# Two layers' causal convolution: one more of four channel tiles per layer as TensorE products (five tiles of eight)

## The chip, the cores and the metric

One core of one Trainium2 chip. The metric is the device time of one execution in microseconds (us), as the median of several runs; less is better. The engines are named TensorE (PE in the profile; its weight loads are PEld), VectorE (DVE), ScalarE (ACT), GpSimd (POOL) and SyncE (SP, which only issues transfers here). Each engine works through its own list of instructions in order; semaphores join them.

## What is computed

512 tokens of width 1024 go through two layers of a conformer-like block (16 learned tokens stand in front, so a layer works on L = 528 positions; the second layer needs only the last 512, T = 512), and then through one block with windowed attention, gated linear attention and 16 experts. All of it is float32. A layer of the first block, cut to what matters:

```python
a, g, zc, q, k, v, za, qi, ki, wi = split(h @ w_in[l])
u = a * sigmoid(g)                                   # [528, 512]
u = causal_conv(u, conv_w[l], width=31, per channel) + conv_b[l]
y_conv = silu(layer_norm(u)) * silu(zc)
y_attn = sparse_attention(q, k, v, qi, ki, wi, topk=132) * silu(za)
h = layer_norm(alpha * h + concat(y_conv, y_attn) @ w_out[l])
```

The convolution is depthwise: each of the 512 channels has 31 taps of its own, and reaches 30 positions back. The attention chooses 132 keys per query by a score of its own (`qi`, `ki`, `wi`).

## The kernel before, in words

The activations lie transposed, 128 channels on the partitions and the positions along the row, as a high and a low float32r part. A projection of 128 output channels (`proj`, line 164) is 8 blocks of the contraction times 3 products (high by high, low by high, high by low) times 2 column pieces: 48 matmuls at line 182 into one of two rotating accumulators named `pp`. Its weights are loaded by SP into one of three `raw` buffers, and split into `wh` on ScalarE (line 160) and `wl` on VectorE (line 161).

`layer` (line 281) writes a layer down phase by phase in the order `seq` of the plan (lines 75 to 86). `idx`, `sc` and `topk` are the key selection, with `topk` wholly on VectorE; `q`, `k`, `v`, `za`, `zc` are projections; `att` is the attention, one query block of 128 after another in four steps and more; `agN` computes the gated input of convolution tile N. A framework decides what comes first on each engine: every instruction has a priority by its level (`go`), the levels are ordered by the first tuple of the plan, and the framework lays out each engine's list by priority among what is ready in a simulation that it makes while it builds. In layer 0 `w`, `topk` and `tail` come ahead of `idx`, `proj`, `conv`, `att`, `ag`, `rest`; in layer 1 `w` and `tail` come ahead of `idx`, `conv`, `proj`, `att`, `ag`, `topk`, `rest`. Buffers of one name ("tag") rotate in the order in which the program is written, whatever the priorities are.

A convolution tile is 128 channels. `p_ag` (line 378) makes two projections (`a` and `g`), a tanh `th` on ScalarE (line 385) and one multiply on VectorE (line 386), which writes the tile's input `u`. The last entry of the plan, `pconv`, says which tiles then go tap by tap; their projections stand at level `ag`, those of the others at `proj`:

- Tap by tap (`conv_tap`, line 328): for each of 31 taps ScalarE scales a shifted view of `u` by the tap into one of two `prod` buffers (line 333), and GpSimd adds it to `cv` (line 335). The first tap writes `cv` itself, with the bias. So a tile is 31 activations and 30 adds.
- As products (`conv_operands`, line 341, and `conv_products`, line 363): the 128 channels are four groups of 32. TensorE spreads the taps over partitions with 16 small matmuls (line 346), VectorE turns them into diagonal weights `cwt` (line 348, buffer `k2l`). SP writes `u` to DRAM (`ud`, line 354) and reads it back four times per group, each time shifted by one position more, onto the four quarters of the partitions (`us` in the buffer of `szc`, line 359, and `side`, line 360). Then eight products per group, each of four taps for 32 channels, add up in `pp`; the four groups' products write four quarters of 32 output channels. These are two bursts (one per half of the columns) of 32 matmuls each (`burst`, lines 253 to 267, so they appear at lines 261 and 267), and ScalarE takes the result to `cv` with the bias (line 376). An fp32 product leaves two records in the trace.

Before, layer 0 makes tile 3 as products and tiles 0, 2 and 1 tap by tap (tile 0 at the very start of the layer, 2 and 1 during attention); layer 1 makes tiles 2 and 3 as products and 1 and 0 tap by tap, during attention.

The tail follows (line 712). First comes a warm-up: ScalarE reads the last tile of the sequence (`clast`, line 713, used at line 722) and then computes a square root (line 723), so that the table for it is loaded. Then `cv` is transposed (line 727), copied (`xct`, line 729) and measured (line 730), normalised, transposed back (line 754), passed through silu (line 755) and multiplied by `szc` (line 756) into `ych` and `ycl`. `xct` takes over buffers named `pT` that attention uses before. The attention output is multiplied into the gate `sza` (line 551) and split into `yah` and `yal`. The output projection (`w_out`, from line 766) reads `yah`, `yal` first and `ych`, `ycl` after them. Attention itself: scores on TensorE (`pidx`), mask and maximum on VectorE (`smb`, `mx`, lines 646 and 648), exponentials on ScalarE (line 651), transposes (line 616), copies (line 618) and products with the values (`po`).

Of the kernel before, what the change touches and what calls it, by code (L numbers as in the profile page):

```python
# [69 lines left out]
class Net:  # L70
    def __init__(self, tc, I, out, dbg=None, upto=99):
        self.tc, self.nc, self.I, self.out, self.dbg = tc, tc.nc, I, out, dbg
        self.upto = upto
        self.bgq = []
        self.plan = [
            (('w', 'topk', 'tail', 'idx', 'proj', 'conv', 'att', 'ag', 'rest', 'fill'),
             ('ag0', 'idx', 'q', 'k', 'sc', 'ag3', 'v', 'cp3', 'ag2', 'ag1', 'topk', 'zc', 'att', 'za'),
             (2, 0, 1, 3),
             (2, 3, 1, 0),
             (0, 1, 2)),  # L80
            (('w', 'tail', 'idx', 'conv', 'proj', 'att', 'ag', 'topk', 'rest', 'fill'),
             ('idx', 'q', 'k', 'sc', 'ag2', 'v', 'cp2', 'ag3', 'ag1', 'cp3', 'ag0', 'topk', 'att', 'za', 'zc'),
             (2, 0, 1, 3),
             (2, 3, 1, 0),
             (0, 1)),
        ]
        self.order2 = ('w', 'crit', 'att', 'gla', 'main', 'late', 'fill')
        self.gn0, self.apull, self.gpull, self.ng = 2, 3, (1, 0, 2, 1), 0
        self.early = ("qk", "qk", "u", "szc", "cv", "qi", "xl", "xl", "parts", "v", "c1", "sm", "sm", "one", "raw", "raw", "raw", "hw", "hl")
        self.last = ("raw", "u", "szc", "qi")  # L90
        self.cycle = ("qk", "qk", "u", "szc", "cv", "qi", "xl", "xl", "v", "sm", "sm", "one", "raw", "raw", "raw", "hw", "hl")
        self.piece = 264
        self.swap = True
        self.stack = True
        self.sqsum, self.sqe, self.xlp = 'v', 'AAAAAAAA', ()
        self.pairs2 = False
        self.pairs, self.spare = False, None
        self.cur = None
        self.pos = 0
# [181 lines left out]
    def layer(self, l):  # L281
# [46 lines left out]
        def conv_tap(c, j):  # L328
            src = u[:, c, j + 1 + q0:j + 1 + q0 + T]
            if not prod:  # L330
                prod.append(self.sb([128, 2, L], "prod", "zM"))
            pr = prod[0][:, j % 2, :T] if j else cv[:, c, :]
            nc.scalar.activation(pr, src, AF.Identity, scale=taps[:, c, j + 1:j + 2], bias=0.0 if j else cvec[:, c, 31:32])  # L333
            if j:
                nc.gpsimd.tensor_tensor(cv[:, c, :], cv[:, c, :], pr, op=ALU.add)  # L335
# [5 lines left out]
        def conv_operands(c):  # L341
            nx = T + W31 + 1 - CQ
            pt = self.ps([128, 4, 8], "pcv")
            for g in range(4):
                for k in range(CQ):
                    nc.tensor.matmul(pt[32 * k:32 * k + 32, g, :], self.ident[:, 32 * g:32 * g + 32], taps[:, c, k::CQ], start=True, stop=True)
            w = self.sb([128, 4, 8, 32], "cwt", "k2l")
            nc.vector.tensor_tensor(w.rearrange("p g e c -> p (g e) c"), self.mask32[:, None, :].to_broadcast([128, 32, 32]),
                                    pt.rearrange("p g e -> p (g e)")[:, :, None].to_broadcast([128, 32, 32]), op=ALU.mult)

            ust = self.sb([128, 3, nx], "us", "szc")
            us = [ust[:, g, :] for g in range(3)] + [self.side[:, 32:32 + nx]]
            ud = self.dram.tile([128, PAD + L], F32, name=f"ud{l}{c}")
            nc.sync.dma_start(ud, u[:, c, :])
            ug = ud.rearrange("(g p) x -> p g x", g=4)
            for k in range(CQ):
                p = slice(32 * k, 32 * k + 32)
                x0 = k + q0
                nc.sync.dma_start(ust[p], ug[:, 0:3, x0:x0 + nx])
                nc.sync.dma_start(us[3][p], ug[:, 3, x0:x0 + nx])  # L360
            ready[c] = w, us

        def conv_products(c):
            self.go("proj")
            n = T // 2
            w, us = ready.pop(c)
            ps = self.ps([128, 2, 512], "pp", "pp", 2)
            for k in range(2):
                products = []
                for e in range(8):  # L370
                    for g in (3, 2, 1, 0):
                        x0 = CQ * e + n * k
                        products.append(((ps[32 * g:32 * g + 32, k, :n], w[:, g, e, :], us[g][:, x0:x0 + n]),
                                         dict(start=e == 0, stop=e == 7, skip_group_check=True)))
                self.burst(products)
            nc.scalar.activation(cv[:, c, :].rearrange("p (k n) -> p k n", k=2), ps[:, :, :n], AF.Identity, scale=1.0, bias=cvec[:, c, 31:32])

        def p_ag(c):
            self.go("ag" if c in pconv else "proj")
            ps = []  # L380
            for n in ("a", "g"):
                raw = self.load_w(w_in, WCOL[n] + 128 * c, 128)
                ps.append(self.proj(self.split_w(raw), 128, hT, KT, fsegs))
            th = self.sb([128, L], "th", "rl", 3)
            nc.scalar.activation(fseg(th), ps[1], AF.Tanh, scale=0.5)  # L385
            nc.vector.scalar_tensor_tensor(fseg(u[:, c, PAD:]), fseg(th), 1.0, ps[0], op0=ALU.add, op1=ALU.mult)
            if c not in pconv:
                conv_operands(c)
                return
            self.go("conv")  # L390
            for j in range(W31):
                conv_tap(c, j)
# [112 lines left out]
        v = self.sb([128, 4, 512], "v")  # L505
# [199 lines left out]
                tmp = self.sb([128, T], "th", "rl", 3)  # L705
                self.silu2(seg(szc[0][:, e, :]), ps, seg(tmp))

        phases = dict(cp2=lambda: conv_products(2), cp3=lambda: conv_products(3), ag0=lambda: p_ag(0), ag1=lambda: p_ag(1), ag2=lambda: p_ag(2), ag3=lambda: p_ag(3), idx=p_idx, sc=p_scores, topk=p_topk, k=p_k, q=p_q, v=p_v, att=p_att, za=p_za, zc=p_zc)
        for n in seq:
            phases[n]()  # L710

# [73 lines left out]
        sc = self.sb([128, 5, 2], "sc")  # L785
# [1008 lines left out]
```

## Time and profile before

| | |
|---|---|
| Time, median of 3 runs | 1838.72 us (1835.46 to 1839.21) |
| The profiled execution, own time | 1837.06 us |
| Its span from the first to the last instruction | 1835.2 us |
| TensorE busy, share of the span | 1688.8 us, 92% |
| VectorE / ScalarE / GpSimd busy | 931.9 / 766.7 / 219.8 us |
| Mean granted TensorE clock | 0.970 of full speed |
| Layer 0 / layer 1 / the rest, about | 0 to 400 / 400 to 740 / 740 to 1835 us |

Numbers in the profile are microseconds from the start of the span unless marked ns. A matmul's record is longer than the distance to the next one, since they overlap; the distance is what a stream of them takes. "Idle before" is time in which an engine did nothing, with what ended it: `3.31 <-DVE mx L646` says that it waited 3.31 us until VectorE's instruction of line 646 that writes `mx`. Idle time of an engine that is not the bottleneck costs nothing.

### The profile page before, as it was taken

What the parts mean: (1) busy time and instruction counts of PE and PEld (TensorE: products, weight loads), DVE (VectorE), ACT (ScalarE), POOL (GpSimd) and SP (SyncE); (2) the same over time, 40 slices, a digit from 0 to 9 for tenths busy, and PEclk for the clock granted to TensorE, in tenths of its full rate; (3) what the DMA queues carried; (4) which work ended last, traced back from release to release, by engine and by line L of the source; (5) the groups of instructions that cost most, each with busy time, mean ns of one, the idle gap of its engine ahead of it and who ended that gap; (6) DMA issues with size and microseconds to landing.
All of it is one profiled execution on the core that took longest, in us unless ns stands there. A gap on an engine that the chain in (4) does not pass through costs nothing.

```text
span 1835.2 us, 28863 instructions
## 1 busy us (share of the span) xinstructions
PE 1688.8 (92%) x11867; PEld 1320.9 (72%) x11867; DVE 931.9 (51%) x1860; ACT 766.7 (42%) x1314; POOL 219.8 (12%) x161
## 2 busy tenths in 40 slices
PE   6999998989999999799999999998899988788888
PEld 6988896989987879798978899997533333233246
DVE  3899756566995556875534455544311221012044
ACT  3883587356526783643456453323200000000026
POOL 1620486000005740000000000000000000000000
PEclk9999998989999999899999999999999999999999
DMA  6124120121233112222113248466699999999961
GB/s 195 58 70 113 47 70 24 53 71 47 76 97 110 47 47 70 81 92 68 58 47 98 78 158 296 131 247 252 240 420 421 421 420 421 419 420 421 418 272 46
DMA packets 149461, 327.63 MB, mean 179 GB/s; under 512 B 13467, under 2 KB 103259, under 8 KB 131025
## 3 DMA queue, kind: packets, MB, share of 16 engines
q1 hardware_dynamic: 144464, 314.75, 46.7%
q10 hardware_dynamic: 3856, 7.37, 1.1%
q0 software_dynamic: 1008, 3.67, 0.5%
q8 instruction: 93, 1.52, 0.3%
q14 instruction: 40, 0.32, 0.1%
HBM read 308.58 MB, written 17.11 MB: 177 GB/s over the span
## 4 chain that ended last, share of the span: by engine, by line
PE 64%; DMA 17%; ACT 7%; DVE 6%; POOL 3%; issue 2%; ACTq 0%; DVEq 0%; POOLq 0%; SPq 0%
PE pp L182 41%; PE pp L1643 8%; DMA rawe<-in_w_exp_up 6%; DMA rawe<-in_w_exp_down 5%; DMA rawe<-in_w_exp_gate 4%; POOL cv L335 3%; PE pp L1703 2%; ACT wh L160 1%; ACT prod L333 1%; ACT smb L651 1%; PE pidx L242 1%; PE psc L1541 1%; PE po L261 1%; PE pidx L243 1%; DVE wl L161 1%
## 5 line engine op out<-in xcount | busy, mean ns | idle before, releaser
L335 POOL TENSOR_TENSOR cv<-cv,prod 128x528 f32<-128x528 f32 (+1 forms) x150 | 212.9, 1420 | 452.9 <-ACT prod L333 444.8
L1643 PE MATMUL pp<-rawe,xf 128*64 128x512 f32 x1024 | 251.0, 606 | 11.1 <-DMA rawe<-in_w_exp_gate 6.9
L160 ACT CAST wh<-raw 128x1024 fp32r<-128x1024 f32 (+2 forms) x149 | 151.0, 1016 | 253.1 <-PE pp L182 221.2
L182 PE MATMUL pp<-hTh,wh 128*128 128x264 f32 (+2 forms) x1056 | 223.3, 291 | 12.0 <-ACT th L385 9.8
L161 DVE TENSOR_TENSOR wl<-raw,wh 128x1024 fp32r<-128x1024 f32 (+2 forms) x149 | 186.6, 1253 | 92.1 <-ACT wh L160 81.9
L182 PE MATMUL pp<-hTl,wh 128*128 128x264 f32 (+2 forms) x1056 | 221.7, 289 | 0.0
L182 PE MATMUL pp<-hTh,wl 128*128 128x264 f32 (+2 forms) x1056 | 219.9, 287 | 0.0
L1643 PEld LDWEIGHTS pp<-rawe,xf 128*64 128x64 f32 x1024 | 78.4, 139 | 158.7 <-issue 133.0
L182 PEld LDWEIGHTS pp<-hTh,wh 128*128 128x128 f32 (+1 forms) x1056 | 165.4, 190 | 22.1 <-ACT th L385 12.2
L182 PEld LDWEIGHTS pp<-hTl,wh 128*128 128x128 f32 (+1 forms) x1056 | 165.7, 189 | 6.0 <-issue 5.5
L182 PEld LDWEIGHTS pp<-hTh,wl 128*128 128x128 f32 (+1 forms) x1056 | 165.5, 190 | 4.5 <-issue 4.0
L182 PE MATMUL pp<-xTh,wh 128*128 128x264 f32 (+1 forms) x752 | 153.7, 285 | 2.9 <-ACT op L1072 2.3
L182 PE MATMUL pp<-xTl,wh 128*128 128x264 f32 (+1 forms) x752 | 154.9, 285 | 0.7 <-DVE xTl L1167 0.7
L182 PE MATMUL pp<-xTh,wl 128*128 128x264 f32 (+1 forms) x752 | 154.5, 283 | 0.0
L1643 PE MATMUL pp<-rawe,hid 128*64 128x512 f32 x512 | 127.8, 617 | 19.1 <-DMA rawe<-in_w_exp_down 18.7
L1532 DVE SCALAR_TENSOR_TENSOR Y<-pp,per,Y 128x512 fp32r<-128x512 f32 x16 | 12.0, 748 | 233.5 <-ACT Y L1531 233.5
L333 ACT ACTIVATE prod<-u,taps 128x528 f32<-128x528 f32 (+1 forms) x150 | 107.3, 729 | 36.5 <-POOL cv L335 35.9
L1500 POOL DMA_INDIRECT xr<-xrows,slots x7 | 6.7, 958 | 938.8 <-DMA pled<-pe 639.4
L182 PEld LDWEIGHTS pp<-xTh,wh 128*128 128x128 f32 (+1 forms) x752 | 115.2, 189 | 4.6 <-ACT op L1072 2.5
L182 PEld LDWEIGHTS pp<-xTl,wh 128*128 128x128 f32 (+1 forms) x752 | 115.0, 188 | 3.6 <-issue 2.5
L182 PEld LDWEIGHTS pp<-xTh,wl 128*128 128x128 f32 (+1 forms) x752 | 115.1, 188 | 0.8 <-issue 0.8
L1643 PEld LDWEIGHTS pp<-rawe,hid 128*64 128x64 f32 x512 | 40.2, 141 | 100.6 <-issue 62.7
(526 smaller groups left out, 2941.7 us busy)
## 6 DMA issues: line engine op xcount, KB each, us to landing
rawe<-in_w_exp_gate SPq DMA_DIRECT2D x53, 1024.0 KB
rawe<-in_w_exp_up SPq DMA_DIRECT2D x52, 1024.0 KB
rawe<-in_w_exp_down SPq DMA_DIRECT2D x51, 1024.0 KB
raw<-in_w_in SPq DMA_DIRECT2D x45, 1024.0 KB
rawe<-in_w_exp_down SPq DMA_DIRECT2D x26, 512.0 KB
rawe<-in_w_exp_up SPq DMA_DIRECT2D x22, 512.0 KB
rawe<-in_w_exp_gate SPq DMA_DIRECT2D x22, 512.0 KB
raw<-in_w_in SPq DMA_DIRECT2D x20, 512.0 KB
```

What stands on the lines that cost most here:

```text
L160: nc.scalar.copy(wh, raw_view)
L161: nc.vector.tensor_sub(wl, raw_view, wh.bitcast(F32))
L182: nc.tensor.matmul(ps[:m, s, x:min(x + k, n)], a[:, t, :m], b[:, c0 + x:min(c0 + x + k, c1)], start=(t == 0 and pi == 0 and x == 0), stop= ...
L242: nc.tensor.matmul(out, qs[:, p, x, :], kh, start=True, stop=False)
L243: nc.tensor.matmul(out, qs[:, p, x, :], kl, start=False, stop=True)
L261: first = self.nc.tensor.matmul(*args, **kw)
L333: nc.scalar.activation(pr, src, AF.Identity, scale=taps[:, c, j + 1:j + 2], bias=0.0 if j else cvec[:, c, 31:32])
L335: nc.gpsimd.tensor_tensor(cv[:, c, :], cv[:, c, :], pr, op=ALU.add)
L651: nc.scalar.activation(sm[:, x, :], sm[:, x, :], AF.Exp, bias=mx[:, h:h + 1], scale=0.125, accum_out=ssum[:, h:h + 1])
L1541: nc.tensor.matmul(ps, ohts[j][:, 128 * i:128 * (i + 1)], Ys[j][:, k, s * 512:(s + 1) * 512], start=(k == 0), stop=(k == 1))
L1643: nc.tensor.matmul(ps[a, s, :], x[:, a], r, start=(t == 0 and k == 0), stop=(t == KT - 2 and k == 1), skip_group_check=True)
L1703: nc.tensor.matmul(ps[k][:, k, :], a[:, t, :], wp[t][:, w, k * 512:(k + 1) * 512], start=(t == 0 and pi == 0), stop=(t == KT - 1 and pi == 2))
```

## The change

In layer 0 tile 2 goes as products instead of tap by tap, in layer 1 tile 1. So tap by tap remain tiles 0 and 1 in layer 0 and tile 0 in layer 1. The order of the phases changes with it: in layer 0 `ag1` now stands ahead of `ag2`, and `cp2` behind it; in layer 1 `ag0` stands ahead of `ag1`, which moves behind `cp3`, with `cp1` behind it. The projections of the two moved tiles go from level `ag` to level `proj`. The last tile of the sequence, which the tail's warm-up reads, becomes tile 2 in layer 0 (it was 1) and tile 1 in layer 1 (it was 0). No function gets another body; two names are added to the table of phases.

```diff
         self.plan = [
             (('w', 'topk', 'tail', 'idx', 'proj', 'conv', 'att', 'ag', 'rest', 'fill'),
-             ('ag0', 'idx', 'q', 'k', 'sc', 'ag3', 'v', 'cp3', 'ag2', 'ag1', 'topk', 'zc', 'att', 'za'),
+             ('ag0', 'idx', 'q', 'k', 'sc', 'ag3', 'v', 'cp3', 'ag1', 'ag2', 'cp2', 'topk', 'zc', 'att', 'za'),
              (2, 0, 1, 3),
              (2, 3, 1, 0),
-             (0, 1, 2)),
+             (0, 1,)),
             (('w', 'tail', 'idx', 'conv', 'proj', 'att', 'ag', 'topk', 'rest', 'fill'),
-             ('idx', 'q', 'k', 'sc', 'ag2', 'v', 'cp2', 'ag3', 'ag1', 'cp3', 'ag0', 'topk', 'att', 'za', 'zc'),
+             ('idx', 'q', 'k', 'sc', 'ag2', 'v', 'cp2', 'ag3', 'ag0', 'cp3', 'ag1', 'cp1', 'topk', 'att', 'za', 'zc'),
              (2, 0, 1, 3),
              (2, 3, 1, 0),
-             (0, 1)),
+             (0,)),
         ]
...
-        phases = dict(cp2=lambda: conv_products(2), cp3=lambda: conv_products(3), ag0=lambda: p_ag(0),
...
+        phases = dict(cp0=lambda: conv_products(0), cp1=lambda: conv_products(1), cp2=lambda: conv_products(2),
...
```

## Rows read from the trace of the kernel before

**Rows 1.** The page, busy time, share of the span and instructions of each engine.

```profile
PE 1688.8 (92%) x11867; PEld 1320.9 (72%) x11867; DVE 931.9 (51%) x1860; ACT 766.7 (42%) x1314; POOL 219.8 (12%) x161
```

**Rows 2.** Table by stretch: from:to, length, busy time (instructions) per engine, clock, DMA.

```profile
core 0: us, PE busy (x) PEld busy (x) DVE busy (x) ACT busy (x) POOL busy (x), PEclk, DMA share, GB/s
204.00:291.00 87.00, 85.28 (x750) 77.19 (x749) 49.39 (x132) 70.77 (x147) 69.30 (x50) 1.00 0.18 59
291.00:317.00 26.00, 18.86 (x131) 12.73 (x129) 17.19 (x39) 19.11 (x38) 14.81 (x11) 0.80 0.03 11
317.00:345.00 28.00, 23.79 (x165) 23.31 (x166) 16.07 (x32) 14.67 (x26) 0.00 (x0) 0.82 0.05 12
...
600.00:679.00 79.00, 76.86 (x672) 68.96 (x671) 42.96 (x98) 61.41 (x128) 51.70 (x38) 0.98 0.16 54
679.00:700.00 21.00, 16.66 (x122) 15.88 (x121) 13.77 (x24) 16.23 (x23) 0.00 (x0) 0.92 0.00 1
```

**Rows 3.** TensorE's waits, 291 to 345 us: for what, us in total, times, longest.

```profile
PE pp L182 <- DVE ycl L197: 3.5, 1, 3.5
PE tp L616 <- DVE mx L646: 3.3, 1, 3.3
PE pp L182 <- ACT yah L196: 1.8, 1, 1.8
PE pidx L267 <- DVE mx L648: 1.2, 1, 1.2
PE tp L727 <- DVE cst L730: 1.0, 1, 1.0
```

**Rows 4.** TensorE's waits, 545 to 700 us, the six largest.

```profile
PE pp L182 <- ACT th L385: 3.5, 1, 3.5
PE pp L182 <- ACT yah L196: 1.4, 1, 1.4
PE pp L182 <- DVE ycl L197: 1.4, 1, 1.4
PE pp L261 <- ACT th L385: 1.2, 1, 1.2
PE tp L616 <- ACT smb L651: 1.1, 1, 1.1
PE pp L182 <- DVE yal L197: 0.9, 1, 0.9
```

**Rows 5.** Taps, whole span: ns min/median/max, forms; last row: ScalarE's waits at line 333.

```profile
L333 ACT ACTIVATE prod<-u,taps x150: 705/728/767, 38.8 to 663.6; 128x528 f32<-128x528 f32 x90, 128x512 f32<-128x512 f32 x60
L335 POOL TENSOR_TENSOR cv<-cv,prod x150: 1269/1316/2712, 39.6 to 664.9; 128x528 f32<-128x528 f32 x90, 128x512 f32<-128x512 f32 x60
...
  POOL cv L335: 35.9, 48
```

**Rows 6.** Timeline of TensorE: start, us; a burst's begin, what follows it, small products.

```profile
178.52 0.41 PE L261 MATMUL pp<-side,cwt 128*32 128x264 f32 x1
...
182.10 0.60 PE L267 MATMUL psm<-qk,kmb 128*32 128x512 f32 x3
...
547.13 0.44 PE L346 MATMUL pcv<-taps,base 128*32 128x8 f32 x32
```

**Rows 7.** Timeline of SP, layer 0: first, second and last transfer of tile 3.

```profile
152.35 0.34 SPq L354 DMA_DIRECT2D ud<-u  x1
154.78 0.34 SPq L359 DMA_DIRECT2D us<-ud  x1
...
157.98 0.43 SPq L360 DMA_DIRECT2D side<-ud  x1
```

**Rows 8.** The chain that ended last, one projection of 48 matmuls: start, us, what.

```profile
159.51 5.85 PE pp L182 x48
```

**Rows 9.** Timeline of ScalarE, the warm-up's table load in layer 0.

```profile
310.41 1.28 ACT L723 ACT_TABLE_LOAD   x1
```

**Rows 10.** Timeline of VectorE, the multiplies into the attention gate in layer 0.

```profile
295.73 4.63 DVE L551 TENSOR_TENSOR sza<-yas,sza 128x512 f32<-128x512 f32 x3
...
312.63 0.63 DVE L551 TENSOR_TENSOR sza<-yas,sza 128x512 f32<-128x512 f32 x1
```

More of the change, by code (lines that the diff above doesn't have):

```diff
@@ L706, in p_zc @@
                 self.silu2(seg(szc[0][:, e, :]), ps, seg(tmp))
-        phases = dict(cp2=lambda: conv_products(2), cp3=lambda: conv_products(3), ag0=lambda: p_ag(0), ag1=lambda: p_ag(1), ag2=lambda: p_ag(2), ag3=lambda: p_ag(3), idx=p_idx, sc=p_scores, topk=p_topk, k=p_k, q=p_q, v=p_v, att=p_att, za=p_za, zc=p_zc)
+        phases = dict(cp0=lambda: conv_products(0), cp1=lambda: conv_products(1), cp2=lambda: conv_products(2), cp3=lambda: conv_products(3), ag0=lambda: p_ag(0), ag1=lambda: p_ag(1), ag2=lambda: p_ag(2), ag3=lambda: p_ag(3), idx=p_idx, sc=p_scores, topk=p_topk, k=p_k, q=p_q, v=p_v, att=p_att, za=p_za, zc=p_zc)
         for n in seq:
```

## The prediction

> **What bounds the kernel now.** I read four views, in this order: the busy times of the page, a table by stretch, the waits of TensorE in the two places where it waits, and the durations of the instructions that the change removes and adds.
>
> TensorE is busy for 92% of the span [rows 1], so the first question is where it isn't. The table by stretch [rows 2] covers the second half of both layers: in layer 0 from the first tap of the late tiles (204 us) to the output projection, in layer 1 the same from 545 us. In the long middle stretches TensorE is nearly gapless: 85.3 of 87 us and 76.9 of 79 us. Here ScalarE has 70.8 of 87 us and GpSimd 69.3, so both are heavily used, but whatever they delay, TensorE fills with projections of lower priority. The ends are different: from 291 to 317 us TensorE has 18.9 of 26 us at a granted clock of 0.80, from 317 to 345 us 23.8 of 28 at 0.82, from 679 to 700 us 16.7 of 21 at 0.92. So a chain through GpSimd and ScalarE exists, but it is not alone: TensorE's own work is nearly as long, and time can only be won in its holes.
>
> The holes by what ended them: in layer 0 five waits with 10.8 us in sum, first on the last attention steps (3.3 and 1.2), then on the tail of the convolution branch (1.0, 1.8, 3.5) [rows 3]. In layer 1 the six largest have 9.5 us: 3.5 for the gate `th` of the last tap tile, 1.2 and 1.1 behind ScalarE, and 1.4, 1.4 and 0.9 at the start of the output projection [rows 4]. To these comes TensorE at a part of its clock, the mean of its two levels (1.2 and 2.4 GHz) in the stretch: 0.18 of 28 us is 5.0 us in layer 0, 0.08 of 21 us is 1.7 us and 0.02 of 79 us is 1.6 us in layer 1 [rows 2]. All that can be won is 10.8 + 9.5 + 8.3 = 28.6 us.
>
> **What the change removes.** Per layer 30 adds on GpSimd at 1.316 us median and 31 ScalarE activations at 0.728 us: 39.5 us of GpSimd, 22.6 us of ScalarE [rows 5]. All of it lies beside TensorE's work and gives nothing directly. ScalarE also stood 35.9 us behind GpSimd in the whole kernel (two product buffers, so the third product waits for the first add) [rows 5]. With one tile fewer the last half of each attention runs free of this, and since attention has priority over the projections, it ends earlier against them.
>
> **What it adds.** 64 fp32 products per tile on TensorE, in two bursts. The second burst of layer 0 goes from 178.52 to 182.10, when the next group starts: 3.58 us [rows 6]. Two are 7.2 us at 264 columns and 6.9 at 256 (by columns). The 16 small products for the weights take half of the 0.44 us that a row with 32 records shows (a product of this type leaves two records), 0.2 us; I take the full 0.4 as a bound. Sum 7.6 + 7.4 = **15.0 us**. It falls where TensorE has no gaps, so it counts in full. The evacuation of the tile on ScalarE and the weight tile on VectorE, one instruction each, I cost at nothing: the projections in TensorE's list cover them, and without that cover they would stand ahead of the burst, like the operands below.
>
> Nine transfers per layer join SP's queue. For the tile that does this today the first is issued at 152.35, the next, which waits for it, at 154.78, the last at 157.98 [rows 7]; with the 2.1 us that the first needed after its issue, the operands are there some 8.2 us after the first issue. In the kernel before, projections of `v` or another gate lie between a tile's gate and its products. Now `cp2` (layer 0) and `cp1` (layer 1) stand right behind their gate in the program, and the projections' accumulators have two buffers in rotation, so one projection (48 products, 5.85 us [rows 8]) fits between. Weight loads queued on SP behind the first transfer wait with it, for at most the same 8 us, under which three raw buffers stand. Bounds per layer: 0 where attention fills it, 8.2 - 5.9 = 2.3 us where nothing does. I take 0.5, nearer to 0, since attention's products are ready in both places.
>
> One step moves without being meant: the tail's warm-up (line 722) waits for the last tile of the sequence. That was the last tap; now it is a product tile that is done early, and the tail stands above attention in both orders. The warm-up's table load takes 1.28 us [rows 9]. Between attention's exponentials it could cost two loads there and another one in the tail. Bounds: 0 and 3 x 1.3 = 3.9 us per layer; I take 0.65, since only the load in the tail has nothing beside it.
>
> **What it gives back.** Layer 0: the two attention waits (4.5 us) go. They stand behind VectorE, whose three multiplies into `sza` took 4.63 us while GpSimd was adding, and 0.63 us for one after the last add [rows 10]; 4.63 - 3 x 0.63 = 2.7 us is the stretch beside GpSimd. Of the tail's 6.3 us of waits and 5.0 us of lost clock I take three quarters, 8.5: attention ends earlier against the projections, but the tail's own transposes still follow attention, because its tiles take over attention's buffers. Layer 1: the 3.5 us behind `th` with its 1.6 us of clock, and the 1.2 us, may return, since tile 1's gate now stands behind tile 0's taps as tile 0's did behind tile 1's; half, 3.1. The 1.1 us goes; of 1.4 + 1.4 + 0.9 + 1.7 three quarters, 4.1. Sum 13.0 + 8.3 = **21.3 us**.
>
> The Trainium skill (Trainium Architecture — The Big Picture, the corrections on SBUF) says that GpSimd and VectorE contend for one port pair, by an exclusive lock. The two multiplies' rows agree with it; no run here separates the lock from other causes.
>
> **The sum.** 15.0 + 1.0 (operands) + 1.3 (tables) - 21.3 = -4.0 us. Against the profiled execution (span 1835.2, own time 1837.06) this is 1833.1; the median of the runs shown is 1.7 us higher, so **1834.7 us**. 0.2% (3.7 us) is about what a measurement of this kernel can tell from no change.
>
> **The rivals.**
> - *TensorE pays and gets nothing back.* The work goes onto the busiest engine, and the holes hang on attention's last steps and on the tail's chain, which still begins after attention. Then the time is 1838.7 + 15.0 = 1854, with both side costs 1856; with attention's waits alone recovered (4.5 + 1.1), 1850. It decides as soon as less than 15 us of the 28.6 return. For it: attention's own chain is unchanged, and `cp2`, `cp1` have priority over it. Against it: the clock and the waits fail only where ScalarE or VectorE was late. 0.29. The Trainium skill (Perfetto Trace Analysis, Identifying the Most-Contended Engine) speaks for this one: the engine with the highest occupancy is to be relieved first. By it alone the sum would be +15. The same section judges TensorE by its weight loads; here they take 77.2 of 87 us [rows 2], still the most of any engine.
> - *All holes close.* ScalarE with 22.6 us less lets attention end so early that the whole tail lies beside the last projections: 15.0 - 28.6 = -13.6, 1825. For it: GpSimd and ScalarE have 0.80 and 0.81 of the middle stretch. 0.20.
> - *The operands come late.* The products stand at the head of TensorE's order while the transfers run: 2 x 2.3 us and as much again at the lower clock, on top of the forecast: about 1844. 0.10.
> - The forecast, most holes closed, 1829 to 1839: 0.41.
>
> **How the numbers follow.** The time is the forecast's. The range goes from 2 us below the closed holes to the first rival with a part of attention's waits: 1823 to 1850; outside lie some 0.18. Faster by over 0.2%: the closed holes and a little over half of the forecast (0.20 + 0.24), 0.44. The same: the rest of the forecast and the milder half of the late operands (0.17 + 0.05), 0.22. Slower: 0.29 + 0.05 = 0.34.
>
> **What would show it.** In the changed trace GpSimd has 90 adds for 150, TensorE two more groups of 128 records at line 267. Right: attention's exponentials end before the last projection of the input, and the waits for `yah`, `ych` and `ycl` are gone from both layers. Wrong: output projections that start 7 us later in each layer with the same waits; a table load amid attention; a hole in front of the added bursts.

## The result and the profile after

The changed kernel takes **1852.47 us** (median of 4 runs, 1850.62 to 1856.97), beside 1838.12 us for the kernel before in the same session: ratio **1.0079 [1.0062, 1.0096]**, slower. The forecast was 1834.7 us with a range of 1823 to 1850, so it was wrong in sign and size. The profiled execution took 1850.62 us, with a span of 1848.8.

The page's busy times, which answer to [rows 1]:

```profile
PE 1704.6 (92%) x12187; PEld 1329.0 (72%) x12187; DVE 922.0 (50%) x1862; ACT 732.8 (40%) x1256; POOL 138.2 (7%) x101
```

The work moved as described: GpSimd has 81.6 us less, ScalarE 33.9 less, TensorE 320 records more (two tiles of 160). So the question is only where TensorE's time went. Three first instructions divide the span: line 818 (layer 0's last transposes) moved from 388.0 to 393.9 us, line 1160 (the same behind layer 1) from 742.7 to 760.5, line 1643 (the first experts) from 1310.2 to 1325.2. In these two executions layer 0 lost 5.9 us and layer 1 11.9. The second block, which the change does not touch, took 4.2 us less, so the span grew by 13.6.

The table by stretch, which answers to [rows 2]; the columns are the same. First the second half of both layers as a whole (up to a point in the output projection behind its last wait, as in [rows 2]), then their parts:

```profile
204.00:351.00 147.00, 135.65 (x1173) 117.67 (x1173) 78.93 (x205) 89.99 (x185) 42.98 (x30) 0.92 0.16 49
540.00:718.00 178.00, 163.54 (x1566) 139.56 (x1556) 93.30 (x252) 95.01 (x186) 40.42 (x30) 0.98 0.22 67
...
205.00:226.00 21.00, 16.84 (x109) 12.21 (x108) 14.09 (x38) 15.92 (x37) 16.26 (x11) 0.84 0.43 118
226.00:236.00 10.00, 10.00 (x141) 5.57 (x141) 2.21 (x3) 5.11 (x8) 8.76 (x7) 0.83 0.01 3
240.00:297.00 57.00, 57.00 (x511) 52.50 (x512) 29.59 (x89) 34.18 (x79) 15.95 (x12) 1.00 0.17 57
297.00:322.00 25.00, 21.99 (x208) 18.20 (x206) 16.21 (x43) 13.73 (x28) 0.00 (x0) 0.99 0.14 44
322.00:351.00 29.00, 24.82 (x168) 24.34 (x169) 15.78 (x29) 16.08 (x27) 0.00 (x0) 0.77 0.05 11
594.00:613.00 19.00, 8.34 (x71) 5.56 (x73) 8.77 (x17) 14.48 (x28) 17.83 (x13) 0.82 0.47 128
613.00:620.00 7.00, 7.00 (x130) 4.63 (x128) 0.00 (x0) 1.45 (x2) 4.29 (x4) 1.00 0.01 2
624.00:700.00 76.00, 76.00 (x664) 66.99 (x663) 38.73 (x118) 38.89 (x94) 0.00 (x0) 1.00 0.17 56
700.00:718.00 18.00, 16.15 (x134) 15.51 (x133) 11.26 (x20) 12.49 (x18) 0.00 (x0) 1.00 0.00 1
```

The reader is to see that the late stretches did become denser (624 to 700 us without a gap, the tail of layer 1 with 1.9 us idle instead of 4.3), and that new holes, stretches in which TensorE stands idle, lie earlier: 205 to 226 us in layer 0, and 594 to 613 us in layer 1, where TensorE is busy for 8.3 of 19 us. The same stretches of the kernel before, as a whole:

```profile
204.00:345.00 141.00, 127.92 (x1044) 113.23 (x1044) 82.64 (x202) 104.54 (x209) 84.11 (x60) 0.93 0.13 41
540.00:700.00 160.00, 148.74 (x1348) 131.44 (x1347) 94.05 (x233) 112.22 (x215) 80.95 (x60) 0.98 0.21 65
```

As an estimate, count as lost what TensorE is idle plus what it misses of the full clock, (1 - clock) times the length. Layer 0: before 13.1 + 0.07 x 141 = 23.0 us, after 11.4 + 0.08 x 147 = 23.1. Layer 1: before 11.3 + 3.2 = 14.5, after 14.5 + 3.6 = 18.0 (clocks have two decimals, so each sum is good to 0.8 us). The forecast wanted 19.0 us less of it (21.3 back, 2.3 of side costs); it got none in layer 0 and 3.5 more in layer 1. So the products are paid, and nothing comes back.

TensorE's waits, layer 0 from 172 to 351 us and then layer 1 from 551 to 718, which answer to [rows 3, 4]:

```profile
PE pp L182 <- DVE ycl L197: 3.5, 1, 3.5
PE pp L182 <- ACT yah L196: 2.8, 1, 2.8
PE po L261 <- ACT pT L618: 2.1, 1, 2.1
PE pp L261 <- DMA side<-ud: 2.0, 1, 2.0
...
PE pidx L261 <- ACT pT L618: 6.9, 1, 6.9
PE po L261 <- ACT pT L618: 2.1, 2, 1.5
PE pp L261 <- DMA side<-ud: 2.1, 1, 2.1
PE pp L182 <- DVE ycl L197: 1.2, 1, 1.2
PE tp L616 <- ACT smb L651: 1.1, 1, 1.1
```

In layer 0 the waits of attention's last steps (3.3 and 1.2) are gone, the tail's are not (3.5 as before, and 2.8 where it was 1.8). In layer 1 the 3.5 behind `th` is replaced by 6.9 behind `pT`, and a wait for the transfers (2.0 and 2.1) stands in front of each added burst.

How the 6.9 us come about is read from ScalarE's timeline; the last column is its idle time and what ended it:

```profile
593.91 0.72 ACT L333 ACTIVATE prod<-u,taps 128x512 f32<-128x512 f32 x1
595.07 0.72 ACT L333 ACTIVATE prod<-u,taps 128x512 f32<-128x512 f32 x1 [0.44 <-POOL cv L335]
597.27 0.72 ACT L333 ACTIVATE prod<-u,taps 128x512 f32<-128x512 f32 x1 [1.48 <-POOL cv L335]
598.62 0.72 ACT L333 ACTIVATE prod<-u,taps 128x512 f32<-128x512 f32 x1 [0.62 <-POOL cv L335]
599.25 1.03 ACT L160 CAST wh<-raw 128x1024 fp32r<-128x1024 f32 x1
600.18 0.60 ACT L385 ACTIVATE th<-pp 128x528 f32<-128x528 f32 x1
600.68 0.71 ACT L333 ACTIVATE prod<-u,taps 128x512 f32<-128x512 f32 x1
601.29 0.84 ACT L618 COPY pT<-tp 128x384 f32<-128x384 f32 x2
```

The moved tile's gate ends on TensorE at 594.3, and the transposes that `pT` copies at 595.0. ScalarE could serve both then, but in its list three scaled taps of tile 0 stand ahead of them, each waiting for GpSimd's add. So `th` comes at 600.2 and `pT` at 601.3; with `th` late, `u` is late, and the transfers that need it too. TensorE's and SyncE's timelines:

```profile
594.14 0.82 PE L616 MATMUL tp<-base,smb 128*128 128x128 f32 x6
601.81 1.00 PE L261 MATMUL pidx<-qk 64*128 64x384 f32 x1 [6.86 <-ACT pT L618]
...
612.73 0.40 PE L261 MATMUL pp<-side,cwt 128*32 128x256 f32 x1 [2.07 <-DMA side<-ud]
```

```profile
602.99 0.34 SPq L354 DMA_DIRECT2D ud<-u  x1
605.85 0.33 SPq L359 DMA_DIRECT2D us<-ud  x1
...
609.03 0.43 SPq L360 DMA_DIRECT2D side<-ud  x1
```

The last transfer is issued 6.0 us after the first, about as for tile 3 before (5.6 in [rows 7]), and the burst begins 9.7 us after the first. Between the gate and the burst TensorE's list holds attention alone, no projection, although projections were left to do: in the list the burst stands ahead of them.

### The profile page after: what moved, and what is told of

Its sections match the earlier page's. It is cut to its first block, busy times and chain, and to the rows that moved or that the text cites. A ratio compares the mean times of both kernels' runs of the same rounds, so it can differ in the third digit from the quotient of the medians.

```text
span 1848.8 us, 29381 instructions
## 1 busy us (share of the span) xinstructions
PE 1704.6 (92%) x12187; PEld 1329.0 (72%) x12187; DVE 922.0 (50%) x1862; ACT 732.8 (40%) x1256; POOL 138.2 (7%) x101
## 4 chain that ended last, share of the span: by engine, by line
PE 67%; DMA 19%; DVE 5%; ACT 5%; issue 2%; POOL 1%; SPq 0%; ACTq 0%; DVEq 0%; POOLq 0%
PE pp L182 42%; PE pp L1643 7%; DMA rawe<-in_w_exp_down 6%; DMA rawe<-in_w_exp_up 5%; DMA rawe<-in_w_exp_gate 4%; PE pp L1703 2%; PE pp L267 1%; POOL cv L335 1%; DMA rawe<-in_w_ple_gate 1%; PE pidx L261 1%; PE po L261 1%; PE pidx L242 1%; PE tp L616 1%; DVE wl L161 1%; PE pidx L243 1%
## 5 line engine op out<-in xcount | busy, mean ns | idle before, releaser
L335 POOL TENSOR_TENSOR cv<-cv,prod 128x528 f32<-128x528 f32 (+1 forms) x90 | 131.3, 1459 | 485.8 <-ACT prod L333 479.2
L1525 ACT COPY hid<-tp 128x512 f32<-128x512 f32 x16 | 8.6, 589 | 188.1 <-PE tp L1523 188.1
```

## The experiments

Each kernel is the changed one with the edit shown; "L0" and "L1" are the lines of the plan for the two layers. Ratios are to the kernel before, timed on the same chip. Lengths of a stage are from one execution each and vary by 2 to 3 us between executions of one plan: layer 0 ended at 387.2 to 389.6 in four kernels that have it as before, at 391.7 to 393.9 in three that have it as changed, and at 383.5 to 386.4 in three in the covered order (the order of *cover_both*, below). The second block varies more: no edit touches its code, and it took 1085.7 to 1096.7 us. So verdicts go by the ratios.

**Two theories.** The first: TensorE simply pays 15 us for the products, wherever they stand (the first rival). The second: the loss comes from where they stand, right behind their gate and its transfers, at the head of the list.

*cover_both* puts other work between gate and products (in layer 0 it also puts `zc` behind `za`).

```diff
-L0 'ag1','ag2','cp2','topk','zc','att','za'
+L0 'ag1','ag2','topk','att','za','cp2','zc'
-L1 'ag0','cp3','ag1','cp1','topk','att','za','zc'
+L1 'ag0','cp3','ag1','topk','att','za','cp1','zc'
```

> Theory L (late operands): in the changed kernel the added products stand at the head of TensorE's list while their operands are still on the way (waits for side of 2.0 and 2.1 us, and around them 205 to 226 us and 594 to 613 us with 16.8 of 21 and 8.3 of 19 us busy at a clock of 0.84 and 0.82). With the gate's projections (za) between the gate of the tile and its products in both layers, both stretches become dense; the 15 us of products remain, most of the old holes stay closed: 1836 to 1842. Theory P (TensorE pays): the loss is the 15 us of products themselves on the busiest engine; where they stand is of no matter: 1850 to 1855.

Measured: 1834.39 us, **0.998 [0.9964, 0.9996]**, still below the range of theory L. The same products, 18 us less than the changed kernel. Its table by stretch, with the two added bursts in the second and third row and the two layers ahead and behind:

```profile
204.00:340.50 136.50, 127.58 (x1156) 114.05 (x1155) 75.71 (x199) 87.95 (x181) 41.87 (x30) 0.96 0.17 52
...
246.00:253.00 7.00, 7.00 (x128) 5.59 (x128) 2.23 (x5) 4.72 (x12) 5.88 (x5) 1.00 0.45 152
...
621.00:628.00 7.00, 7.00 (x129) 4.01 (x125) 0.00 (x0) 0.00 (x0) 0.00 (x0) 1.00 0.04 10
...
540.00:702.50 162.50, 152.01 (x1491) 130.03 (x1490) 86.26 (x228) 92.52 (x185) 40.61 (x30) 1.00 0.24 73
```

The bursts stand in gapless stretches at the full clock, 7.4 and 7.1 us long. The lost time is 8.9 + 5.5 = 14.4 us in layer 0 (23.1 in the changed kernel) and 10.5 in layer 1 (18.0): 16 of the 18 us. The first theory falls.

*layer0_only* and *layer1_only* change one layer as the change does and leave the other as before.

```diff
 layer0_only:
-L1 'ag3','ag0','cp3','ag1','cp1','topk'   taps (0,)
+L1 'ag3','ag1','cp3','ag0','topk'   taps (0, 1)
 layer1_only:
-L0 'ag1','ag2','cp2','topk'   taps (0, 1)
+L0 'ag2','ag1','topk'   taps (0, 1, 2)
```

> Layer 0 as changed, layer 1 as before. In the changed trace the last transposes of layer 0 begin 5.9 us later than before (393.9 for 388.0). Theory L: the hole of layer 0 is the smaller one, so about a third of the loss: 1842 to 1845. Theory P: half of the 15 us: 1845 to 1847.

> Layer 1 as changed, layer 0 as before. In the changed trace layer 1 loses 11.9 us more (first transposes behind it at 760.6 for 742.8, less the 5.9 of layer 0). Theory L: two thirds of the loss and the hole of 594 to 613 us in the trace: 1846 to 1850. Theory P: half of the 15 us: 1845 to 1847.

Measured: layer 0 alone 1.0002 [0.9988, 1.0016], below both theories, layer 1 alone 1.0060 [1.0042, 1.0078], theory L. Most of the loss is layer 1's; its hole is the same there, 6.8 us behind `pT` and 2.1 for the transfers. Of layer 0's later end (392.4 in this execution) nothing clear of the noise is left in the time.

*no_transfer*: the moved tile's products read the operands of the tile before it, and its own nine transfers are left out.

```diff
+            if c == 2 - l:
+                ready[c] = w, self.us_last
+                return
             ust = self.sb([128, 3, nx], "us", "szc")
...
             ready[c] = w, us
+            self.us_last = us
```

> The changed kernel with the moved tile's products reading the operands that the tile before left in us and side, so its own nine transfers per layer are left out (tile 2 of layer 0 and tile 1 of layer 1 are computed from the wrong tile's input); all products remain. Theory L: without the wait for the transfers the two stretches become dense: 1836 to 1843. Theory P: 1850 to 1855, since TensorE does the same work. If it falls between, say 1845 to 1849, the hole hangs on the gate's th behind ScalarE's taps as well, not on the transfers alone.

Measured: 1856.99 us, 1.0108 [1.0079, 1.0138], above every range named and no faster than the changed kernel. Layer 0 ended at 388.9 where the changed layer 0 ends at 391.7 to 393.9: there the transfers cost 3 to 5 us. Layer 1 was no shorter (368.1 us long, 366.6 in the changed kernel). Its largest wait between 540 and 640 us (line 389 of this kernel is line 385 of the others), and two stretches of it, the hole and the tail:

```profile
PE pp L261 <- ACT th L389: 5.6, 1, 5.6
```

```profile
588.00:612.00 24.00, 18.04 (x210) 12.57 (x208) 7.62 (x14) 17.93 (x32) 19.42 (x15) 0.93 0.15 44
...
690.00:718.00 28.00, 22.02 (x152) 21.19 (x153) 17.09 (x33) 14.85 (x23) 0.00 (x0) 0.88 0.07 22
```

Without transfers the burst moved up to its gate, and then needed the accumulators that `th` frees: a hole behind ScalarE is there without any transfer. What the transfers cost in layer 1 this run does not tell. The hole got smaller (7.6 us lost, 14.1 from 594 to 613 in the changed kernel), and the tail lost 9.3 us where the changed kernel loses 1.9. So time won at a hole is not yet won for the layer. The second block took 8 us longer than in the changed kernel (1096.7 and 1088.2); why is not shown.

*one_tap_layer1* takes away what ScalarE is held at: in layer 1 tile 0 makes only its first tap.

```diff
-            for j in range(W31):
+            for j in range(1 if l else W31):
```

> The changed kernel, but in layer 1 the one tile that is left to taps makes only its first tap: 30 activations on ScalarE and 30 adds on GpSimd are left out there. The products with their place in the order and their nine transfers stay. Theory S, layer 1 loses its time because ScalarE stands behind GpSimd at tile 0's taps and so hands th and pT over late: the 6.9 us hole of TensorE in front of the attention's scores at 595 us is gone or below 2 us, layer 1 is 9 to 13 us shorter, and the time 1840 to 1844. Theory O, the order alone is at fault (products right behind their gate, with 8 us of transfers, whatever ScalarE does): holes of 4 us and more remain there, and the time stays at 1848 to 1852.

Measured: 1846.16 us, 1.0040 [1.0023, 1.0056], 2 us above the range of theory S and below that of theory O. Layer 1 was 8.4 us shorter (358.2), where theory S gave 9 to 13. Its waits between 540 and 640 us:

```profile
PE pp L261 <- DMA side<-ud: 2.6, 1, 2.6
PE po L261 <- ACT pT L618: 1.5, 1, 1.5
PE pidx L261 <- ACT pT L618: 1.2, 1, 1.2
```

The hole of 6.9 us is down to 1.2, as theory S said, and the wait for the transfers stays. So ScalarE, held at tile 0's taps by GpSimd, makes the hole.

**What the products themselves cost.** *half_products* (covered order) leaves out half of the moved tile's products in both layers, *eighth_products_layer0* seven eighths in layer 0, on top of *layer0_covered* (layer 0 covered, layer 1 as before). The edit of half_products; for seven eighths the number is 1, in layer 0 alone:

```diff
+                ne = 4 if c == 2 - l else 8
-                for e in range(8):
+                for e in range(ne):
...
-                                         dict(start=e == 0, stop=e == 7, skip_group_check=True)))
+                                         dict(start=e == 0, stop=e == ne - 1, skip_group_check=True)))
```

> cover_both, but the moved tile of each layer makes only the first four of its eight products per group, so 16 of its taps are left out and its two bursts have 16 matmuls each instead of 32. Everything else stays, operands and transfers included. What is left out takes 3.6 us of TensorE per layer. Theory F, in a dense stream TensorE's work counts in full in both layers: 1834.4 - 7.2 = 1827 (1825.5 to 1828.5). Theory G, it counts in layer 1 alone, and in layer 0 the attention and the tail set the end: 1834.4 - 3.6 = 1831. Theory H, it is hidden in both: 1834 to 1835.

> Layer 0 with its moved tile as products, but in the order topk, att, za, cp2, zc (as in cover_both); layer 1 as in the kernel before. Theory A, the layers add: layer 0 ends 4 to 5 us earlier than in the kernel before (383.5 against 388.0 in cover_both), layer 1 lasts about 355 us as before, and the time is 1838 - 4.5 = 1833.6 (1831 to 1835): about 0.9975 of the kernel before, and no worse than cover_both. Theory B, the gain of layer 0 is lost again in the second block, which took 563.8 us behind layer0_only's late first block and 567.4 in the kernel before: the first block ends some 4 us earlier and the time is still 1837 to 1838.

> layer0_covered, but the moved tile of layer 0 makes only the first of its eight products per group: 28 taps are left out, 56 of 64 products, 7/8 of 7.3 = 6.4 us of TensorE. Operands, transfers and order stay. Theory F, the products count in full: 1834 - 6.4 = 1827.5, ratio 0.9940. Theory G, in layer 0 they fill time that TensorE would lose to attention's end and the tail: 1833 to 1834, ratio 0.9970 to 0.9975. Half of it between: 0.9958.

Measured: half_products 0.9956 [0.9942, 0.9970], 4.4 us below cover_both, nearest to theory G (3.6); the two intervals make the difference uncertain by some 4 us, so theory F (7.2) is not excluded by this run. layer0_covered 0.9975 [0.9964, 0.9987] (1833.93 us), the time of theory A. eighth_products_layer0 0.9987 [0.9976, 0.9997], 2 us above layer0_covered, uncertain by 3: 6.4 us of TensorE's work less in layer 0 and no gain. The second half of layer 0, first in layer0_covered, then in eighth_products_layer0:

```profile
204.00:343.00 139.00, 130.07 (x1181) 116.16 (x1180) 78.45 (x209) 90.53 (x186) 43.08 (x30) 0.98 0.17 51
```

```profile
204.00:342.00 138.00, 125.46 (x1066) 111.75 (x1065) 80.45 (x209) 90.14 (x186) 43.64 (x30) 0.96 0.17 52
```

The lost time rose from 8.9 + 2.8 = 11.7 us to 12.5 + 5.5 = 18.0, about as much as the work fell. So in the covered order layer 0's products fill time that TensorE would otherwise lose. What layer 1's products cost there these runs leave open.

But theory A's layer 1 was wrong. In its order of before, layer 1 lasts 354.5 and 354.7 us behind the layer 0 of layer0_only and of the kernel before, and 360.3, 360.3 and 359.9 us behind the covered one (layer0_covered, eighth_products_layer0, layer0_covered_warm). In the profiled executions the two layers end at 746.0 us in layer0_covered and at 744.7 in layer0_covered_warm, later than the 742.7 of the kernel before, while both kernels are 3 to 5 us faster than it. So the gain of the covered order over the kernel before is measured, but not traced to a place in the two layers.

**The warm-up.** *warm_up_on_taps* lets it read the last tap tile again, *warm_up_late* the last output of attention, *layer0_covered_warm* the same on layer0_covered.

```diff
 warm_up_on_taps:
-        clast = int([n for n in seq if n.startswith("ag")][-1][2])
+        clast = 1 - l
 warm_up_late, layer0_covered_warm:
-        nc.scalar.activation(warm, cv[:, clast, 0:1], AF.Abs)
+        nc.scalar.activation(warm, yas[tseq[-1] // 2][:, tseq[-1] % 2, 0:1], AF.Abs)
```

> The changed kernel, but the tail's warm-up reads the last tap tile again (tile 1 in layer 0, tile 0 in layer 1), not the moved tile. Theory W, the table loads that the earlier warm-up brings amid attention are paid in full: the page has two loads fewer, 2 x 1.28 us, and the time is 1852.5 - 2.6 = 1850 (1848.5 to 1850.5). Theory N, they lie beside TensorE's work: the time stays at 1852 to 1853.

> The changed kernel, but the tail's warm-up reads the last output of attention (yas), so the square root's table is loaded behind attention's last exponentials and not amid them. The run on the last tap tile only moved the early loads (from 237 to 256 us in layer 0) and took none away, so the question is still open. Theory W, the tail pays: of the two loads that stand one behind the other in each layer's tail (lines 277 and 734 at 324 and 325 us) one goes, 1.28 us per layer: 1852.5 - 2.6 = 1850 (1.0065 of the kernel before, after 1.0079). Theory N, the loads lie beside TensorE's work: the time stays at 1852 to 1853.

> layer0_covered with the warm-up of warm_up_late, as the candidate that should beat both kernels. Theory W, one table load of 1.28 us less in each tail: 1834 - 2.6 = 1831.4, ratio 0.9961. Theory N: 1834, ratio 0.9975. If the later warm-up holds up the tail's copies on ScalarE instead, 1835 to 1837.

Measured: 1.0081 [1.0064, 1.0099], but this edit told nothing: with one tap tile fewer the tap tiles are done early as well, layer 0's load only moved from 237 to 256 us and none went. warm_up_late has two loads per layer where the changed kernel has four; 1.0067 [1.0053, 1.0082] fits the 2.6 us of theory W, but its interval overlaps the changed kernel's. layer0_covered_warm gave 0.9983 [0.9974, 0.9992], no gain (layer 1 kept its four loads there). So whether the loads cost time is left open: the difference is 2 us, uncertain by 4. The kernel before has two loads in layer 0 and four in layer 1, so the change added two in layer 0 and none in layer 1.

**Layer 1 settled.** *layer1_covered* has layer 1 as in cover_both, but layer 0 as before.

```diff
-L0 'ag1','ag2','cp2','topk'   taps (0, 1)
+L0 'ag2','ag1','topk'   taps (0, 1, 2)
-L1 'ag0','cp3','ag1','cp1','topk','att','za','zc'
+L1 'ag0','cp3','ag1','topk','att','za','cp1','zc'
```

> Layer 1 with its moved tile as products in the covered order (as in cover_both), layer 0 as in the kernel before. Theory F, in layer 1 the covered products are paid in full and nothing is given back, as the stage's length says (361.7 us in cover_both, 354.7 in the kernel before): 1838.3 + 7 = 1845, ratio 1.0038. Theory G, they are given back in that layer or behind it, as the difference of cover_both (0.998) and layer0_covered (0.9975) says: 1838 to 1840, ratio 1.0000 to 1.0008.

Measured: 1.0045 [1.0032, 1.0058], theory F's number; yet behind the covered layer 0 the same order cost 1 us (0.998 against 0.9975). The layers do not add, and the waits from 540 to 640 us show one reason. First cover_both, then layer1_covered:

```profile
PE pp L182 <- ACT th L385: 2.5, 1, 2.5
PE po L261 <- ACT pT L618: 1.5, 1, 1.5
```

```profile
PE pp L182 <- ACT th L385: 5.9, 1, 5.9
PE po L261 <- ACT pT L618: 1.5, 1, 1.5
PE pp L182 <- ACT cv L376: 0.4, 1, 0.4
```

The framework laid out other lists behind the other layer 0: on ScalarE `th` of the moved tile stands behind 20 of tile 0's 31 taps, as in the changed kernel, and behind 17 in cover_both. Against layer1_only's 1.0060 the covered order gains 3 us here, uncertain by 4: in layer 1 the second theory does not hold as it stands. That leaves the gate behind the taps. So the gate was taken out from behind the taps: *early_layer1* (layer 0 covered) and *early_layer1_only* (layer 0 as before) put gate and products of tile 1 around `k`, before any tap of tile 0.

```diff
-L1 'q','k','sc','ag2','v','cp2','ag3','ag0','cp3','ag1','cp1','topk'
+L1 'q','ag1','k','cp1','sc','ag2','v','cp2','ag3','ag0','cp3','topk'
```

> Layer 0 covered as in layer0_covered; in layer 1 the gate of the moved tile 1 stands ahead of k and its products behind k, so both are done before the first tap of tile 0, and no gate stands behind taps on ScalarE. Theory S, layer 1 loses its time where a tanh or a copy on ScalarE stands behind tile 0's taps: no wait of TensorE for th or pT above 2 us is left between 540 and 640 us (2.5 in cover_both, 5.9 in layer1_covered, 6.9 in the changed kernel), and the time is that of layer0_covered plus 7 for the products less the 3.5 of the hole in the kernel before: 1834 + 3.5 = 1837 at most, 1832 to 1837, ratio 0.997 to 0.9995. Rival K, the key selection is what counts: it starts some 19 us later behind the gate and the products, attention follows it, and the layer is 8 us longer or more: 1842 and above, ratio over 1.002.

> The same layer 1 behind layer 0 of the kernel before. Theory S: no hole behind th in layer 1 whatever layer 0 does, unlike the covered order, which had 2.5 us behind one layer 0 and 5.9 behind the other; layer 1 costs the products less the hole of before, 0 to 4 us: 1838 to 1842, ratio 1.000 to 1.002, clearly below layer1_covered's 1.0045. Rival M, the loss of layer1_covered has nothing to do with the hole (it comes from the tail and the clock behind a longer layer): ratio 1.004 and above here too.

Measured: early_layer1 1832.79 us, **0.9968 [0.9958, 0.9978]**, the best of all; early_layer1_only 1.0014 [1.0002, 1.0027]. Both times are where theory S put them; rivals K and M fall. Waits of early_layer1 from 540 to 640 us, and its layer 1 as a stretch:

```profile
PE pp L182 <- DVE rs L673: 1.6, 1, 1.6
```

```profile
540.00:701.50 161.50, 155.75 (x1471) 132.82 (x1470) 100.91 (x267) 95.94 (x191) 38.64 (x30) 0.99 0.23 68
```

No wait for `th` or `pT` is left there, and the lost time is 5.8 + 1.6 = 7.4 us, 14.5 before and 18.0 in the changed kernel. Layer 1 lasts 357.8 us: 3.1 more than before, near the 7.3 of the products less the 3.5 of the old hole. The same five tiles of eight as products are thus 20 us faster than in the change, and 6 us faster than the kernel before. Of the 20 us 16 lie in the layers, which end at 744.2 us instead of 760.5. The 6 us do not: the layers of the kernel before end at 742.7 us, and its second block took 5.8 us longer in its one profiled execution (1092.4 and 1086.6). Where this gain comes from is not shown.

## Why the prediction was wrong, step by step

The step that failed is the one on what comes back: 21.3 us were forecast, with 2.3 us of side costs, and on balance nothing came. By the estimate of lost time three terms of the sum are off by 7 to 11 us each, and each alone would have turned the forecast of -4.0 us.

- **Products, 15.0 us.** Right as a duration where they run undisturbed (7.4 and 7.1 us in cover_both; the forecast's 7.6 and 7.4 have 0.4 for the small products in them). In the change layer 0's burst took 9.2 us, since it began at the lower clock (0.57 from 226 to 230 us); layer 1's took 7.3. "It falls where TensorE has no gaps, so it counts in full" gives the total of the change, but it is no property of the products: in layer 0's covered order seven eighths less of them gained nothing.
- **Operands, 1.0 us, bounds 0 to 2.3 per layer.** This term failed. I took 0.5 "since attention's products are ready in both places". They were there, but they are a chain of short steps through ScalarE and VectorE: TensorE had 16.8 of 21 us at a clock of 0.84 in layer 0 while it waited. With the burst behind it, 9.3 us are lost there (205 to 236 us), where the whole stretch from 204 to 291 us lost 1.7 before. Leaving the transfers out ended layer 0 earlier by 3 to 5 us. The bound assumed that a projection (5.85 us) or attention covers the time in full; the lists put no projection there.
- **Layer 1's gate, "half, 3.1" back.** This term failed most. I named the condition (tile 1's gate behind tile 0's taps, as tile 0's stood behind tile 1's) and then took half a gain. Instead the hole grew from 3.5 to 6.9 us, since `th` and `pT` stood behind taps that waited for GpSimd, and transfers of 9.7 us were chained to it. That the products stood behind the gate in place of projections is not what made it: in layer1_covered, with projections there, it is 5.9. 14.1 us are lost from 594 to 613 us, where the prediction counts 3.5 + 1.6 + 1.2 = 6.3 before. With only the first of tile 0's taps layer 1 is 8.4 us shorter. The bound should have reached below zero.
- **The rest given back.** Layer 0's tail is the third term that failed. Attention's waits in layer 0 (4.5 us) went, and the three multiplies into `sza` fell as priced, by 2.7 us:

```profile
313.67 1.89 DVE L551 TENSOR_TENSOR sza<-yas,sza 128x512 f32<-128x512 f32 x3
```

  They took 4.63 in [rows 10]. The Trainium skill (Trainium Architecture — The Big Picture, the corrections on SBUF) says that VectorE and GpSimd contend for one port pair, by an exclusive lock. These rows agree with it, and no run here separates the lock from other causes. With attention's waits also 5.0 us of lost clock went (0.80 over 26 us before, 0.99 over 25 after), which the sum had not counted. Layer 1's tail gave 4.2 us (idle and clock 6.0 before, 1.9 after), forecast 4.1. Layer 0's tail, forecast at 8.5, gave nothing (9.2 us lost before, 10.9 after): 3.5 + 2.8 us of waits and a clock of 0.77 over 29 us, and the 3.5 for `ycl` is the same in cover_both and early_layer1. The chain behind attention did not get shorter: from the start of the last exponential to line 818 it took 84 us before (303.8 to 388.0) and 87 after (307.1 to 393.9).
- **Table loads, 1.3 us.** Two more loads came, in layer 0 alone. What they cost is not shown (warm_up_late).
- **The rivals.** "TensorE pays and gets nothing back" gave 1850 to 1856, and the time fell there; it had 0.29 and deserved more. That is luck as far as its reason goes. Its mechanism did not hold: the same work on TensorE in another order is faster than before. For it stood a rule of the Trainium skill (Perfetto Trace Analysis, Identifying the Most-Contended Engine), to relieve the engine with the highest occupancy first. Its +15 us is near the 14.4 measured for the change; early_layer1, with the same work on TensorE and 6 us faster than the kernel before, does not follow it. "The operands come late" was right that the products stand at the head of TensorE's list while the transfers run, but it left ScalarE out and was too small: 2.3 us per layer, where TensorE was idle for 4.2 and 10.7 us (205 to 226 and 594 to 613 us). Of "all holes close" the tail of layer 1 came true.

Of the forecast's signs, layer 0's last exponential did come ahead of the last input projection (it began at 307.1 us, the projection's last matmul at 310.5; before the change at 303.8 and 288.8). The waits for `yah` and `ycl` did not go in layer 0 (2.8 and 3.5); in layer 1 those for `yah` and `yal` went and 1.2 us for `ycl` stayed. The hole in front of the added bursts and a table load amid attention, two of the signs of being wrong, did appear.

## What to carry to other kernels

When work moves to another engine, ask first what stands right behind its producer in each in-order list, and what the producer itself stands behind. Here two small steps on ScalarE (`th` and `pT`), behind taps that wait for GpSimd, held TensorE for 6.9 us, about as long as a tile's products take. Put the producer ahead of such a chain, and a full-length piece of ready work between it and its consumer, transfers included: in early_layer1 the same work is 20 us cheaper than in the change. "Something is ready" is not cover unless that something can run densely by itself.

## What was not expected of the hardware

The same 64 products took 7.4 us in a stretch that was dense before (clock 1.00 from 234 to 253 us in cover_both) and 9.2 us in the changed kernel's layer 0, where the granted clock was 0.84 in the 21 us ahead and 0.83 over the burst. There a hole on TensorE was paid twice: 4.2 us of waiting, and 1.8 us in the burst that followed. It is no rule: layer 1's burst came behind a larger hole (10.7 us idle of 19) and ran at a clock of 1.00, in 7.3 us; its low clock (0.58 from 600 to 606 us) was over by then. And two layers with the same plan are not the same program: behind another layer 0 the framework's lists for layer 1 differ, and with them a hole of 2.5 or 5.9 us.
